# Reordering the Strassen products of a ConvFFN up-projection, and what runs beside them

## The chip, the cores and the metric

The kernel runs on one core of one Trainium2 chip. The metric is the device time of one execution in microseconds (us). The engines are TensorE (PE in the views; PEld is its weight load), VectorE (DVE), ScalarE (ACT), GpSimd (POOL) and SyncE (SP), whose queue issues all the DMA transfers spoken of here. Each engine works through its own instructions in the order in which they stand, and waits at an instruction until what it needs is there.

## The reference, cut to what matters

The whole is one step of a hybrid decoder layer over 1024 prompt tokens and 32 sample tokens (1056 columns). The change touches the last part: the output projection of the cross-attention, the norm before the ConvFFN, its up-projection with a causal depthwise convolution and a SiLU gate, and the down-projection.

```
x = x + cross_attn(rmsnorm(x, norm_xa_w), mem_k, mem_v, xa_w_q, xa_w_o)   # ... @ xa_w_o is "phase e"
def conv_ffn(h, buf, w_up, conv_w, conv_b, w_down):                        # h = rmsnorm(x, norm_ffn_w)
    up = h @ w_up                                                          # 1024 -> 2 * 2816
    up, new_buf = causal_dwconv(up, buf, conv_w, conv_b)                   # width 3
    gate, val = jnp.split(up, 2, axis=-1)
    return (jax.nn.silu(gate) * val) @ w_down, new_buf
x = x + f
y = rmsnorm(x, final_norm_w)
```

## The kernel before, in words

Activations lie with features on the 128 partitions and tokens along the row. Every fp32 product is made of three float32r products: `split` writes a rounded copy (`S.copy`, on ScalarE, L143) and the rest (`V.tensor_tensor`, on VectorE, L144), for weights (`w_raw` into `w_hi` and `w_lo`) and for activations alike.

**Phase e** (`phase_e`, L1394 to L1402) is the output projection, in two halves of the tokens: h = 1 with 544 columns (512 prompt and 32 sample tokens) first, then h = 0 with 512. For each of 8 output tiles m, `gemm` runs 24 matmuls (per piece of at most 512 columns) into a PSUM bank, VectorE adds the bank to the residual `raw` (L1397), ScalarE squares it, VectorE adds the square to `acc` (L268), and the next weight tile is split. Two weight tiles are held at most, so that the third output tile needs the split of its weights.

**Operand sums** (`operands`, L1404 to L1441): the normed half is scaled (L1419) and made into the operands of a Strassen-like product with seven multiplications in place of eight: `B11`, `T1` to `T4`, `B21`, `B22`, each with 4 pieces that are subtracted or added and then split. In the order of the program the calls are `phase_e(1)`, `operands(1)`, `phase_e(0)`, `operands(0)`.

**Up stage**: 22 calls of `up_pair(j)`, each for one tile of the gate and one of the value, 128 features each. A pair has seven steps, one for each product; a step runs 12 matmuls with 272 columns (half 1) and 12 with 256 (half 0). `up_quads` loads the two weight tiles of a pair (`w_raw` with two buffers, and `w_raw2`, named w_raw with a number in the order, with one), builds four weight sums in `ws` (on GpSimd, L1454 to L1459) and splits seven weights. They go by turns to tiles named `w_hi` and `w_lo`, two of each, so that a split waits until the product two back with the same name is done. Products are gathered in PSUM: a pair takes four banks for each half (all eight banks in all); partial results are kept in `c1`, `u2`, `u3`, and `out` writes the four quarters of the pair into `fu` and `fus`. Then the convolution follows (ScalarE L1548 and L1549, VectorE L1551 and L1552), SiLU (L1556), the product of gate and value (L1558), and the write to `h_d` in DRAM.

**Down stage**: `hidden(j)` loads a row tile of `h_d` and splits it; four tiles make a group (groups of 4, 4, 4, 4, 2, 4). `down_all` runs, for each of 8 output tiles m and each of 4 quarters of 264 columns, the matmuls of a group (L1603), and VectorE adds each bank to `x2` (the residual, loaded from DRAM at L1576). The weights come through `weight_tiles` with one tile read ahead.

The order in which instructions of different parts stand in an engine's queue is set by a scheduler from this program; it is shown below where it matters.

## Time and profile before

| what | value |
|---|---|
| median of 3 runs | 2004.17 us (1997.27 to 2010.63) |
| the profiled execution | 2003.78 us, its span 2002.0 us |
| mean granted TensorE clock | 0.97 of full speed |
| instructions | 37716 |

The time of an execution is a little longer than the span of its instructions (here by 1.8 us). Sums below are made against the profiled execution, which lies 0.4 us below the median.

### The profile page before, as it was taken

The numbers are of one execution on the slowest core, as the hardware profiler recorded it, in microseconds if no ns is written. First come the engines' busy times: TensorE is split into PE (matmuls) and PEld (weight loads), VectorE is DVE, ScalarE is ACT, GpSimd is POOL, SyncE is SP. The second block draws the span as 40 slices with busy tenths as digits, with TensorE's granted clock in tenths as the row PEclk, the third lists the DMA queues.
The fourth block names the chain that finished last, engine by engine and source line by source line (L and its number), as shares of the span: only waits on it lengthen the run. The fifth ranks groups of instructions, "written<-read, shape, count | busy, mean of one in ns | idle before, by whom it ended". The sixth has DMA issues, their size and how long they took to land.

```text
span 2002.0 us, 37716 instructions
## 1 busy us (share of the span) xinstructions
PE 1846.5 (92%) x15248; PEld 1632.6 (82%) x15248; DVE 1338.2 (67%) x2711; ACT 790.5 (39%) x1541; POOL 287.9 (14%) x405
## 2 busy tenths in 40 slices
PE   6998999989999999999999787999989999799997
PEld 6887878856777677899768677999889999799997
DVE  5566776777786687556554657777777777655466
ACT  4443334345544445345433324444434344311121
POOL 0021110001110100000000012333333333000001
PEclk9999999979999999999999898999999999899999
DMA  7421113153221223753466231121121122732212
GB/s 255 170 67 41 41 38 107 40 155 128 68 71 51 69 62 110 238 176 127 168 228 213 81 116 50 65 75 65 64 85 66 65 75 71 256 91 87 74 54 88
DMA packets 111599, 207.79 MB, mean 104 GB/s; under 512 B 37760, under 2 KB 51392, under 8 KB 111424
## 3 DMA queue, kind: packets, MB, share of 16 engines
q1 hardware_dynamic: 111424, 205.37, 31.5%
q8 instruction: 120, 1.97, 0.4%
q14 instruction: 55, 0.45, 0.1%
HBM read 166.22 MB, written 39.12 MB: 103 GB/s over the span
## 4 chain that ended last, share of the span: by engine, by line
PE 67%; DVE 13%; issue 7%; ACT 5%; DMA 5%; POOL 2%; SPq 0%; POOLq 0%; ACTq 0%; DVEq 0%
PE ps_g L214 21%; PE ps_m L1527 4%; PE ps_y L214 4%; DVE fo L1551 4%; PE ps_g L1603 3%; PE ps_c L1603 3%; PE ps_g L1527 3%; PE ps_x L1527 2%; PE ps_y L1603 2%; PE ps_c L1527 2%; PE ps_x L1603 2%; ACT fo L1548 1%; POOL ir_r L230 1%; DVE fo L1558 1%; ACT w_hi L143 1%
## 5 line engine op out<-in xcount | busy, mean ns | idle before, releaser
L214 PE MATMUL ps_g<-act,w_hi 128*128 128x272 f32 (+1 forms) x1728 | 428.6, 335 | 3.5 <-DVE raw L1397 3.5
L214 PEld LDWEIGHTS ps_g<-act,w_hi 128*128 128x128 f32 x1728 | 293.6, 192 | 42.2 <-issue 12.2
L143 ACT CAST w_hi<-w_raw 128x1024 fp32r<-128x1024 f32 (+1 forms) x174 | 159.3, 916 | 408.6 <-PE ps_g L214 163.2
L214 PE MATMUL ps_g<-act,w_lo 128*128 128x272 f32 (+1 forms) x864 | 291.2, 337 | 0.3
L144 DVE TENSOR_TENSOR w_lo<-w_raw,w_hi 128x1024 fp32r<-128x1024 f32 (+1 forms) x152 | 168.9, 1111 | 77.9 <-ACT w_hi L143 72.5
L214 PEld LDWEIGHTS ps_g<-act,w_lo 128*128 128x128 f32 x864 | 166.4, 193 | 17.3 <-issue 4.6
L1551 DVE SCALAR_TENSOR_TENSOR fo<-fu,vec,fo 128x1024 f32<-128x1024 f32 x88 | 144.8, 1683 | 10.1 <-ACT fo L1548 10.1
L230 POOL TENSOR_TENSOR ir_r<-ir_v,nhalf 128x8 f32<-128x8 f32 (+3 forms) x20 | 34.0, 1698 | 442.9 <-DVE ir_v L226 399.3
L1527 PE MATMUL ps_m<-act,w_hi 128*128 128x272 f32 x528 | 79.9, 294 | 13.2 <-DVE w_hi L144 12.1
L214 PE MATMUL ps_g<-xq,w_hi 128*128 128x272 f32 (+1 forms) x336 | 88.6, 350 | 0.0
L1527 PEld LDWEIGHTS ps_m<-act,w_hi 128*128 128x128 f32 x528 | 70.3, 190 | 18.1 <-DVE w_hi L144 16.9
L1603 PE MATMUL ps_g<-xq,w_hi 128*128 128x264 f32 x392 | 74.5, 287 | 9.0 <-ACT xq L143 9.0
L1527 PE MATMUL ps_m<-xq,w_hi 128*128 128x256 f32 x528 | 74.2, 283 | 0.0
L1527 PE MATMUL ps_c<-xq,w_lo 128*128 128x272 f32 (+1 forms) x528 | 72.4, 286 | 0.0
L1603 PE MATMUL ps_c<-xq,w_hi 128*128 128x264 f32 x380 | 71.9, 286 | 0.0
L143 ACT CAST w_lo<-ws 128x512 fp32r<-128x512 f32 x22 | 13.7, 621 | 142.5 <-PE ps_c L1527 142.5
L1603 PEld LDWEIGHTS ps_g<-xq,w_hi 128*128 128x128 f32 x392 | 61.9, 191 | 9.2 <-ACT xq L143 9.2
L1527 PE MATMUL ps_x<-xq,w_lo 128*128 128x272 f32 x264 | 40.3, 303 | 30.8 <-DVE u L1534 30.8
L1527 PEld LDWEIGHTS ps_m<-xq,w_hi 128*128 128x128 f32 x528 | 68.3, 191 | 0.0
L1527 PEld LDWEIGHTS ps_c<-xq,w_lo 128*128 128x128 f32 x528 | 68.2, 191 | 0.0
L1454 POOL TENSOR_TENSOR ws<-w_raw 128x512 f32<-128x512 f32 x22 | 45.3, 2061 | 158.0 <-ACT xq L143 156.0
L214 PEld LDWEIGHTS ps_g<-xq,w_hi 128*128 128x128 f32 x336 | 59.2, 194 | 10.1 <-issue 3.3
(634 smaller groups left out, 4450.3 us busy)
## 6 DMA issues: line engine op xcount, KB each, us to landing
w_raw<-i_w_in SPq DMA_DIRECT2D x52, 512.0 KB, 3.3
w_raw<-i_w_up SPq DMA_DIRECT2D x44, 512.0 KB, 3.3
h_d<-fo SPq DMA_DIRECT2D x22, 528.0 KB, 2.6
fo<-h_d SPq DMA_DIRECT2D x22, 528.0 KB, 4.9
w_raw<-i_w_out SPq DMA_DIRECT2D x16, 512.0 KB, 4.4
ck<-i_ck SPq DMA_DIRECT2D x16, 512.0 KB, 4.3
w_raw<-i_xa_w_q SPq DMA_DIRECT2D x16, 512.0 KB, 3.3
ck<-i_cv SPq DMA_DIRECT2D x16, 512.0 KB, 4.3
```

What stands on the lines that cost most here:

```text
L143: S.copy(out=hi, in_=src)
L144: V.tensor_tensor(out=lo, in0=src, in1=hi.bitcast(F32), op=ALU.subtract)
L214: PE.matmul(pt[:, :n], a[:, k], b, start=i == 0, stop=i == 3 * nk - 1)
L230: G.tensor_tensor(out=r[:rows, :n], in0=v[:rows, :n], in1=nhalf[:rows, 0:1].to_broadcast([rows, n]), op=ALU.pow)
L1454: G.tensor_tensor(out=s1, in0=wu[:, 0:4], in1=wu[:, 4:8], op=ALU.add)
L1527: PE.matmul(pt[:, :n], w[:, a], X[name][k][:, b], start=i == 0 and not more, stop=i == 11, skip_group_check=True)
L1548: S.activation(out=o[:, 0:2 * T], in_=ub[i][:, 2:2 + 2 * T], func=AF.Identity, scale=w3[2], bias=vc("fb", mt))
L1551: V.scalar_tensor_tensor(out=o[:, 0:2 * T], in0=ub[i][:, t:t + 2 * T], scalar=w3[t], in1=o[:, 0:2 * T], op0=ALU.mult, op1=ALU.add)
L1558: V.tensor_tensor(out=os_[1], in0=os_[1], in1=os_[0], op=ALU.mult)
L1603: PE.matmul(pt[:, :NW], a[:, k], x[:, b], start=i == 0, stop=i == 3 * n - 1)
```

## The change

Five things are done. (1) The seven products come in another order, B11, B21, T2, T1, T3, T4, B22, and are gathered in three banks for each half: one bank takes B11, T2, T3 and T4 one after the other and ScalarE copies it out after B11, T2 and T3 (`c1`, `u2`, `u3`); B21 and T1 have a bank each, and B22 is added to T1's. (2) The weight sums are made on VectorE, all four `ws` tiles are held. (3) `operands(1)` becomes a generator of which four steps are taken after each output tile of `phase_e(0)`. (4) The sample tokens lie behind the prompt tokens in one `fu` tile, so that the convolution is one instruction of 1072 columns in place of two; the result goes to a tile `fh` of its own. (5) In the last pair `passage` loads and splits the first group of the down stage after steps 0 and 1, and loads `x2` after steps 3 and 4, into the tiles that the products leave. `places` is the list of pools that these tiles are taken from.

```diff
-    NAMES = ("B11", "T2", "T3", "T4", "T1", "B21", "B22")
+    NAMES = ("B11", "B21", "T2", "T3", "T1", "T4", "B22")
...
-        def phase_e(h, oa):
+        def phase_e(h, oa, beside=()):
...
+                for _ in range(4):
+                    next(beside, None)
...
-        def operands(h, raw, root):
+        def operands(h, raw, root, X):
...
-                s1, s2, s3, s4 = (f1.tile([P, 4, P], F32, name="ws", bufs=3) for _ in range(4))
+                s1, s2, s3, s4 = (f1.tile([P, 4, P], F32, name="ws", bufs=4) for _ in range(4))
                 for q in range(7):
-                    if q == 1:
-                        G.tensor_tensor(out=s1, in0=wu[:, 0:4], in1=wu[:, 4:8], op=ALU.add)
-                        G.tensor_tensor(out=s2, in0=s1, in1=wg[:, 0:4], op=ALU.subtract)
...
+                    if q == 2:
+                        V.tensor_tensor(out=s1, in0=wu[:, 0:4], in1=wu[:, 4:8], op=ALU.add)
+                        V.tensor_tensor(out=s2, in0=s1, in1=wg[:, 0:4], op=ALU.subtract)
+                    if q == 3:
+                        V.tensor_tensor(out=s3, in0=wg[:, 0:4], in1=wu[:, 0:4], op=ALU.subtract)
+                        V.tensor_tensor(out=s4, in0=wg[:, 4:8], in1=s2, op=ALU.subtract)
+                    x = (wg[:, 0:4], wg[:, 4:8], s2, s1, s3, wu[:, 4:8], s4)[q]
...
-        X1 = operands(1, raw1, root1)
-        raw0, root0 = phase_e(0, oa0)
-        X0 = operands(0, raw0, root0)
+        raw0, root0 = phase_e(0, oa0, operands(1, raw1, root1, X1))
+        for _ in operands(0, raw0, root0, X0):
+            pass
...
-            pts = [[ps("g") for _ in range(2)] for _ in range(4)]
+            pts = [[ps("g") for _ in range(2)] for _ in range(3)]
...
-(("B11", 0, False), ("T2", 1, False), ("T3", 2, False), ("T4", 2, True), ("T1", 3, False), ("B21", 0, True), ("B22", 3, True))
+(("B11", 1, False), ("B21", 0, False), ("T2", 1, True), ("T1", 2, False), ("T3", 1, True), ("T4", 1, True), ("B22", 2, True))
...
+                    if step_ in (0, 2, 4):
+                        S.copy(out=(c1, u2, u3)[step_ // 2][q], in_=pt[:, :n])
+                    if step_ == 1:
+                        out(0, 0, q, add(c1[q], pt))
                     elif step_ == 4:
-                        out(1, 1, q, add(u3[q], pt))
+                        out(1, 1, q, add(u3[q], pts[2][q]))
                     elif step_ == 5:
-                        out(0, 0, q, copy(pt))
+                        out(1, 0, q, copy(pt))
+                hook(step_)
...
+        def passage(step_):
+
+            if step_ in (0, 1):
+                first.append(hidden(2 * step_))
+                first.append(hidden(2 * step_ + 1))
+            if step_ in (3, 4):
+                for k in range(4 * step_ - 12, 4 * step_ - 8):
+                    t = slot().bitcast(F32).rearrange("p a b -> p (a b)")[:, :NTOK]
+                    nc.sync.dma_start(out=t, in_=x2_d[k])
+                    x2.append(t)
```

**VectorE, at the change from the first half of phase e to the second.** The rows of before, from the norm's root of half 1 on; L1419 scales, L144 splits, L1428 and L1430 are operand sums, and the add of the second half's first output tile (L1397, raw_12155) comes 60 instructions behind the root:

```order
L226 TENSOR_SCALAR ir_v<-ps_c 68x8
L1419 SCALAR_TENSOR_TENSOR raw_11511<-raw_11511,vec,ps_c 128x272
...
L144 TENSOR_TENSOR act<-raw_11834,act 128x272
L144 TENSOR_TENSOR act<-raw_11899,act 128x272
L144 TENSOR_TENSOR act<-raw_11964,act 128x272
L1397 TENSOR_TENSOR raw_12155<-raw_12155,ps_y 128x512
```

The same place now, with L1402 the add of the second half's output tiles and L1427 the scaling:

```order
L226 TENSOR_SCALAR ir_v<-ps_c 68x8
L1402 TENSOR_TENSOR raw_12043<-raw_12043,ps_y 128x512
L1427 SCALAR_TENSOR_TENSOR raw_11511<-raw_11511,vec,ps_c 128x272
...
L144 TENSOR_TENSOR xq<-raw_11704,xq 128x272
L144 TENSOR_TENSOR w_lo<-w_raw,w_hi 128x1024
L1402 TENSOR_TENSOR raw_12119<-raw_12119,ps_g 128x512
L1427 SCALAR_TENSOR_TENSOR raw_11769<-raw_11769,vec,ps_c 128x272
L1427 SCALAR_TENSOR_TENSOR raw_11769<-raw_11769,vec,ps_m 128x272
L268 TENSOR_TENSOR acc<-acc,sq 128x512
```

The first add stands ahead of the operand work, and from then on an add, a weight split and a share of the operand work take turns.

**VectorE, one pair of the up stage, now** (L1567 is the convolution, L1574 and L1575 the product of gate and value, L1533 writes a quarter, L1469 to L1473 are the four weight sums; w_raw_15496 and w_raw_15748 are `w_raw2` of this pair and of the next):

```order
L1567 SCALAR_TENSOR_TENSOR fo<-fu,vec,fo 128x1072 x4
...
L144 TENSOR_TENSOR w_lo<-w_raw_15496,w_lo 128x512
L144 TENSOR_TENSOR w_hi<-ws,w_hi 128x512
L144 TENSOR_TENSOR w_lo<-w_raw,w_lo 128x512
L1469 TENSOR_TENSOR ws<-w_raw_15748 128x512
L1533 TENSOR_TENSOR fu<-u_15628,ps_x 128x272
L1470 TENSOR_TENSOR ws<-ws,w_raw 128x512
L1472 TENSOR_TENSOR ws<-w_raw,w_raw_15748 128x512
L144 TENSOR_TENSOR w_hi<-w_raw,w_hi 128x512
L1533 TENSOR_TENSOR fu<-u_15627,ps_c 128x256
```

The sum L1469 needs the load of `w_raw2` for the next pair, whose buffer is free only after the split of w_raw_15496 three rows ahead of it, and the add of a quarter out of PSUM (L1533) stands behind it. Before, the sums stood on GpSimd, and the adds to c1, u2 and u3 (L1532, L1534) in their place.

**SyncE, from the last pair into the down stage.** Before:

```order
L1584 DMA fo<-h_d 128x1056 x2
L184 DMA w_raw<-i_w_down 128x512 x2
L1559 DMA h_d<-fo 128x1056
L1584 DMA fo<-h_d 128x1056 x8
```

Now (L1585 loads a hidden tile, L1599 x2, L1576 writes h_d):

```order
L184 DMA w_raw<-i_w_down 128x512
L1585 DMA fh<-h_d 128x1056
L1576 DMA h_d<-fh 128x1056
L1585 DMA fh<-h_d 128x1056 x2
...
L1585 DMA fh<-h_d 128x1056
...
L1576 DMA h_d<-fh 128x1056
L1614 DMA o_ffn_p<-fp 128x88
L1615 DMA o_ffn_s<-fs 128x704
L1585 DMA fh<-h_d 128x1056 x2
L184 DMA w_raw<-i_w_down 128x512 x2
```

The four loads of the first group now stand ahead of the last pair's write of h_d; the third and fourth weight tile of the down stage, which stood ahead of that write, stand behind it and behind two more loads.

## Rows read from the trace of the kernel before

**Rows 1.** The page: busy time and share of each engine over the span.

```profile
PE 1846.5 (92%) x15248; PEld 1632.6 (82%) x15248; DVE 1338.2 (67%) x2711; ACT 790.5 (39%) x1541; POOL 287.9 (14%) x405
```

**Rows 2.** Busy time by stretch: start:end, length, busy us (instructions), granted clock, DMA share, GB/s.

```profile
1233.10:1715.25 482.15, 442.87 (x3528) 433.96 (x3527) 364.76 (x566) 196.01 (x357) 176.90 (x248) 1.00 0.21 75
1715.25:1724.00 8.75, 0.00 (x0) 0.00 (x0) 7.57 (x9) 4.78 (x6) 0.00 (x0) 0.77 0.90 319
1724.00:1730.20 6.20, 6.02 (x27) 5.99 (x28) 2.64 (x4) 1.83 (x4) 0.00 (x0) 0.50 0.92 298
1730.20:1745.00 14.80, 14.17 (x116) 13.96 (x116) 12.78 (x25) 7.96 (x14) 0.00 (x0) 1.00 0.85 284
...
1138.20:1153.90 15.70, 0.23 (x1) 0.00 (x1) 14.69 (x41) 9.07 (x25) 0.00 (x0) 0.66 0.00 0
...
1190.20:1233.10 42.90, 31.70 (x183) 27.79 (x182) 32.38 (x75) 16.53 (x43) 8.86 (x14) 0.80 0.13 42
```

**Rows 3.** The chain that ended last: start, length, work; two pairs of the up stage.

```profile
1411.59 2.94 PE ps_g L1527 x24
...
1434.61 2.94 PE ps_g L1527 x24
```

**Rows 4.** Timeline of one pair: start, length, engine, line, operation, [idle before <- releaser].

```profile
1438.52 0.69 DVE L144 TENSOR_TENSOR w_lo<-w_raw,w_lo 128x512 fp32r<-128x512 f32 x1 [1.04 <-ACT w_lo L143]
...
1441.10 2.37 ACT L1548 ACTIVATE fo<-fu,vec 128x1024 f32<-128x1024 f32 x2
...
1442.38 5.43 DVE L1551 SCALAR_TENSOR_TENSOR fo<-fu,vec,fo 128x1024 f32<-128x1024 f32 x3 [0.46 <-ACT fo L1548]
...
1443.37 2.16 POOL L1454 TENSOR_TENSOR ws<-w_raw 128x512 f32<-128x512 f32 x1
...
1443.68 0.63 ACT L1530 COPY c<-ps_g 128x272 f32<-128x272 f32 x2
...
1449.98 1.52 PE L1527 MATMUL ps_m<-act,w_hi 128*128 128x272 f32 x10 [0.43 <-DVE w_hi L144]
...
1453.34 1.77 PE L1527 MATMUL ps_x<-xq,w_lo 128*128 128x272 f32 x12 [1.49 <-DVE u L1534]
```

**Rows 5.** DMA issues of the up stage (1300 to 1690): size, median us to landing.

```profile
w_raw<-i_w_up SPq DMA_DIRECT2D x33, 512.0 KB, 3.3
h_d<-fo SPq DMA_DIRECT2D x17, 528.0 KB, 2.6
```

**Rows 6.** Timeline and, for the last row, chain: second half of phase e, operands, first pair.

```profile
1128.48 0.50 DVE L1419 SCALAR_TENSOR_TENSOR raw<-raw,vec,ps_c 128x272 f32<-128x272 f32 x1 [2.62 <-PE ps_c L252]
...
1153.11 0.67 DVE L1397 TENSOR_TENSOR raw<-raw,ps_y 128x512 f32<-128x512 f32 x1
...
1153.71 1.21 DVE L144 TENSOR_TENSOR w_lo<-w_raw,w_hi 128x1024 fp32r<-128x1024 f32 x1
...
1153.93 1.19 PE L214 MATMUL ps_y<-xq,w_hi 128*128 128x512 f32 x2 [15.50 <-DVE raw L1397]
...
1190.31 0.69 DVE L1397 TENSOR_TENSOR raw<-raw,ps_g 128x512 f32<-128x512 f32 x1 [3.11 <-PE ps_g L214]
...
1197.04 1.41 DVE L1419 SCALAR_TENSOR_TENSOR raw<-raw,vec,ps_c 128x512 f32<-128x512 f32 x2 [1.84 <-PE ps_c L252]
...
1218.17 0.68 DVE L144 TENSOR_TENSOR w_hi<-ws,w_hi 128x512 fp32r<-128x512 f32 x1
...
1184.67 5.61 PE ps_g L214 x24
```

**Rows 7.** Timeline: from the last pair into the down stage.

```profile
1716.87 2.45 SPq L184 DMA_DIRECT2D w_raw<-i_w_down  x2
1717.11 3.68 DVE L1551 SCALAR_TENSOR_TENSOR fo<-fu,vec,fo 128x1024 f32<-128x1024 f32 x3 [0.52 <-ACT fo L1548]
...
1723.70 0.33 SPq L1559 DMA_DIRECT2D h_d<-fo  x1
...
1724.18 0.81 PE L1603 MATMUL ps_g<-xq,w_hi 128*128 128x264 f32 x2 [8.97 <-ACT xq L143]
```

More of the change, by code (lines that the diff above doesn't have):

```diff
@@ L1425, in operands @@
                 put("B11", k, lo[k])
+                yield
             for k in range(4):
                 scale(4 + k)
+                put("B21", k, lo[4 + k])
+                yield
+            for k in range(4):
                 V.tensor_tensor(out=hi[k], in0=hi[4 + k], in1=hi[k], op=ALU.subtract)
-                put("T3", k, hi[k])
                 V.tensor_tensor(out=lo[k], in0=lo[k], in1=hi[k], op=ALU.add)
                 put("T2", k, lo[k])
+                yield
+                put("T3", k, hi[k])
+                yield
             for k in range(4):
@@ L1434, in operands @@
                 put("T1", k, hi[k])
+                yield
+            for k in range(4):
                 V.tensor_tensor(out=lo[k], in0=lo[4 + k], in1=lo[k], op=ALU.subtract)
                 put("T4", k, lo[k])
-            for k in range(4):
-                put("B21", k, lo[4 + k])
+                yield
             for k in range(4):
                 put("B22", k, hi[4 + k])
-            return X
+                yield
         def up_quads():
@@ L1477, in pf_ @@
         def pf_():
[L1478 removed]
+            return ff.tile([P, NU], F32, name="fu", bufs=2)[:, :400]
         fp = ff.tile([P, 44, 2], F32, name="fp")
@@ L1518, in copy @@
                 return op
-            for step_, (name, bank, more) in enumerate((("B11", 0, False), ("T2", 1, False), ("T3", 2, False), ("T4", 2, True), ("T1", 3, False), ("B21", 0, True), ("B22", 3, True))):
+            for step_, (name, bank, more) in enumerate((("B11", 1, False), ("B21", 0, False), ("T2", 1, True), ("T1", 2, False), ("T3", 1, True), ("T4", 1, True), ("B22", 2, True))):
                 w = next(quads)
@@ L1557, in up_pair, with hidden, slot @@
                 os_.append(o)
-            V.tensor_tensor(out=os_[1], in0=os_[1], in1=os_[0], op=ALU.mult)
-            nc.sync.dma_start(out=h_d[j], in_=os_[1])
+            hj = ff.tile([P, NTOK], F32, name="fh", bufs=2)
+            V.tensor_tensor(out=hj[:, 0:2 * T], in0=os_[1][:, 0:2 * T], in1=os_[0][:, 0:2 * T], op=ALU.mult)
+            V.tensor_tensor(out=hj[:, 2 * T:].rearrange("p (b t) -> p b t", t=4), in0=samples_of(os_[1]), in1=samples_of(os_[0]), op=ALU.mult)
+            nc.sync.dma_start(out=h_d[j], in_=hj)
+        NW = NTOK // 4
+        LAST = tuple((i * NW, NW) for i in range(4))
+        x2, first = [], []
+        def hidden(j):
+            o = ff.tile([P, NTOK], F32, name="fh", bufs=2)
+            nc.sync.dma_start(out=o, in_=h_d[j])
+            hh = [slot()[:, :, :2 * NW] for _ in range(2)]
+            for i in range(2):
+                split(hh[i][:, 0], hh[i][:, 1], o[:, 2 * NW * i:2 * NW * i + 2 * NW])
+            return hh
+        def passage(step_):
[7 more added lines that the diff above has]
+                    x2.append(t)
+            if step_ == 6:
+                weights[0] = weight_tiles(down_sources())
+        ga = [xp_tile] * 2 + [act_tile] * 2 + [xp_tile] * 2 + [xe_tile] * 2
+        gb = [xp_tile] * 4 + [act_tile] * 4
+        places = ga + [xp_tile] * 2 + [xe_tile] * 2 + [act_tile] * 2 + [xp_tile] * 2 + gb + ga + gb + ga[:4] + gb
+        def slot():
+            return places.pop(0)()
         for j in range(FT):
-            up_pair(j)
+            up_pair(j, passage if j == FT - 1 else lambda i: None)
         nc.sync.dma_start(out=O["ffn_p"], in_=fp)
@@ L1566, in hybrid_step @@
         rings.update(g="ggyccx", m="mm")
-        weights[0] = weight_tiles(down_sources())
-        slots = [xp_tile, act_tile]
-        def slot():
-            slots.append(slots.pop(0))
-            return slots[-1]()
-        x2 = []
-        for k in range(KT):
-            t = act_tile().bitcast(F32).rearrange("p a b -> p (a b)")[:, :NTOK]
-            nc.sync.dma_start(out=t, in_=x2_d[k])
-            x2.append(t)
-        NW = NTOK // 4
-        LAST = tuple((i * NW, NW) for i in range(4))
-        def hidden(j):
-            o = ff.tile([P, NTOK], F32, name="fo", bufs=4)
-            nc.sync.dma_start(out=o, in_=h_d[j])
-            hh = [xp_tile()[:, :, :2 * NW] for _ in range(2)]
-            for i in range(2):
-                split(hh[i][:, 0], hh[i][:, 1], o[:, 2 * NW * i:2 * NW * i + 2 * NW])
-            return hh
         def hcols(hh, q):
@@ L1618, in hybrid_step @@
             j0 = sum(GR[:g])
-            hs_ = [hidden(j) for j in range(j0, j0 + gn)]
+            hs_ = [hidden(j) for j in range(j0, j0 + gn)] if g else first
             if prev:
```

42 lines of the change are left out of this document (17 added, 25 removed).

## The prediction

> **What bounds the kernel now.** I read the page first: TensorE is busy for 92% of the span, VectorE for 67%, GpSimd for 14% [rows 1]. So a gain can only come out of the 8% in which TensorE stands still, or runs at less than its full clock; I looked for these in the table by stretch [rows 2], and then in the timeline of the places that stand out.
>
> Three places stand out. From the 60% mark on, one pair of the up stage follows another at a steady 482.15 / 21 = 22.96 us with the clock granted in full [rows 2]. The chain shows a step's 24 matmuls in 2.94 us [rows 3], so seven steps need 20.58 us, and 2.38 us of each pair are waits: 0.43 us for a weight split on VectorE and 1.49 us for the add into u3 on VectorE (T4 may not be gathered into the bank before T3 is read out of it), the rest being slow restarts [rows 4]. Both waits end on VectorE, which at that time is in its convolution. Ahead of that, in the second half of phase e, TensorE stands still for 15.50 us at the third output tile: the adds and weight splits that it needs stand behind all of the first half's operand work in VectorE's queue, which runs from 1128.48 to 1153.11 [rows 6], and nothing of TensorE's runs beside it (0.23 us of 15.70) [rows 2]. Last, the way into the down stage: 8.75 us without a matmul, then 6.20 us at a granted 0.50, the 1.2 GHz level [rows 2].
>
> **The change, part by part.**
>
> *Operand sums beside phase e.* VectorE's work does not get less, its order changes. The split of the third weight tile (1153.71 now [rows 6]) moves behind one add, eight scalings and four splits; at 0.35 to 0.5 us each that is 6 us behind 1128.5, so 1134.7, and TensorE's third tile starts 19 us earlier. From there on either engine can be the limit. TensorE's limit: six tiles at 5.61 [rows 6] are 33.7 us, so that the last add would start at about 1169.5 in place of 1190.31: a gain of 20.8. VectorE's limit: the operand work with its waits, 24.6 us, eight adds and eight square sums at 0.67, six splits at 1.21, and the first five of the up stage's sums and splits, at 0.69 [rows 4, 6], are 46.1 us from 1127.8 on, so 1173 for the last add: a gain of 17. The two are so near that they will wait for each other now and then; I take 18.5, and 14 to 21 for the range. The wait added to VectorE's queue, of the very first sum for the load of `w_raw2` in front of phase e, costs nothing: behind it stand the last splits of the attention, and phase e's first adds have their own loads to wait for.
>
> *The first pair.* From the scaling of half 0 (1197.04) to the end of the operand work it is 21.1 us [rows 6], and the same afterwards. From then on the first pair now takes until 1233.1, 14.9 us, in a stretch granted 0.80 [rows 2]. In the new order T1 and T3 can run while T4's and B22's operands are still made, so that two products are left, 5.9 us at full clock; I expect the 1.2 GHz level for a part of it, as now, and 10 us. Gain 5; 0 and 9 are the bounds.
>
> *Up stage, TensorE.* Let t count from a pair's first matmul. T2 (t = 5.9) may be gathered into its bank once ScalarE has copied B11's sum out: ScalarE has two convolution instructions of 1.2 us first, and is through with both copies by t = 4.1. T3 comes 2.9 us after T2, with T1 between. T4 follows T3 directly: its half 1 needs the copy of half 1, made beside T3's half 0 by t = 13.9 (needed at 14.7), its half 0 the copy that stands behind one weight cast, at t = 15.7 (needed at 16.2). So the 1.49 goes, and what is late next has 0.5 us to spare. The copies are 0.3 us each [rows 4], and ScalarE has the room: 196.01 of 482.15 us busy [rows 2].
>
> The Trainium skill, "PSUM — Partial Sum Buffer", section "PSUM bank collisions raise a hardware error", asks that an engine's access to a bank be kept apart from TensorE's by semaphores, bank by bank: with T2, T3 and T4 in one bank each must wait for ScalarE's copy. The wait of 1.49 before T4 is such a one in this trace. By that rule alone the wait stays, only for another engine, and what it would give is the first rival.
>
> *Up stage, VectorE.* It loses two adds for each half (1.6 us), the four short convolution instructions (1.0), and the hindrance by GpSimd: three convolution instructions take 5.43 us while GpSimd makes its sums, and 3.68 in the last pair where it makes none [rows 4, 7], so 1.75. It gains four sums of 128x512, as long as a split of that size, 0.69 [rows 4], 2.8 us at most, and 0.5 us for the wider instructions. From 364.76 / 21 = 17.4 busy [rows 2] it comes to 16.3 of 20.6. It would fit; what matters is its order. The split of the last weight out of `w_raw2` is reached at t = 10.8 (convolution from 2.3 to 7.4, a split, the product, three adds). Only then can the next `w_raw2` be loaded, and 3.3 us after its issue [rows 5], at t = 14.6, the first sum can start. VectorE stands there for 1.4 us with the two adds behind it that B22 waits for. By t = 15.8 and 18.2 both are done; B22's halves need them at 17.6 and 19.1. So a second margin of 0.9 us. TensorE is then not held up anywhere: 20.58 us, 20.65 with a little loss, and 21 pairs give 21 x 2.31 = 48.5. The bounds are 50 (no loss at all) and 25 (half the present wait comes back, 1.1 us, as the rows of the waits show it for one of the two).
>
> *Into the down stage.* Here now 8.75 us without work, 2.9 us by the half clock (27 matmuls in 6.20, where the next row has 116 in 14.17, 0.122 each, so 3.3) and 0.7 us later are lost, 12.35 in all [rows 2]. The change loads the first group early, but a tile `fh` has two buffers, which the h_d writes use too. The second tile's load waits for the write of the pair before (t = 9.7 and 2.6 for the landing [rows 5]), the fourth for the split of the second, at t = 19, and lands 2.5 us after the pair's end. TensorE starts at once, stops some 2 us for the fourth tile, and runs on for the first two output tiles, until 13 us after the pair's end. The third needs weights whose load now stands behind the write of h_d (after the convolution, which the fourth tile's splits hold up: 11 us after the pair's end) and behind a load into the buffer of that write (14.4), where it stood ahead of it (at 1716.87 against 1723.70 [rows 7]). With the landing, the two hidden tiles ahead of it on ScalarE, and its own split, it is ready some 20.5 us after the pair's end. So TensorE stands for 2 and 8 us, and runs slow for a while behind the long stop as it does now, 3 us: 13, against 12.35 lost now. I take a loss of 1 us; the bounds are a gain of 9.4 (all hidden but 3 us) and a loss of 5.
>
> The Trainium skill, "SBUF — State Buffer", section "Summary: rules for kernel authors", puts a transfer out of DRAM at about 358 GB/s. This trace has 284 to 319 GB/s here, at 0.85 to 0.92 of the queues' time [rows 2]; by the page's figure the loads would land about a sixth sooner and the sum would be, as an estimate, 2 us lower. I go by the trace.
>
> The sample columns laid behind the prompt's and the tile `fh` are in the sums of VectorE above; the end of the kernel is not touched.
>
> **The sum.** 18.5 + 5 + 48.5 - 1 = 71, off 2003.8: 1933 us. Against the median of the runs it is the same within 0.4 us.
>
> **The rivals.**
>
> *The wait for a bank or for `w_raw2` stays.* For it speaks that both margins are under 1 us, and that a wait on a load which comes 1 us late is paid in full in every pair. Against it, that every pair begins anew at TensorE's end, so that no lateness adds up. With 1.0 to 1.5 us a pair it is 21 to 31 us less gain: 1954 to 1964. Chance 0.17.
>
> *The way into the down stage is hidden after all*, because the loads land sooner or weights come in time: 9.4 us gained in place of 1 lost, 1922. For it: first group, x2 and two weight tiles are in hand when the pair ends. Against: the place of the third weight's load. Chance 0.13.
>
> *VectorE cannot keep up in phase e.* It has 46 us of work for some 45 us of matmuls there; if each step waits for ScalarE as in the rows of before, or TensorE's clock falls again, half of the gain is left: 1943. Chance 0.09.
>
> *Slower than before.* One mechanism: the next `w_raw2` has only one buffer and is loaded only after t = 10.8; if in the up stage it lands late, VectorE stands with B22's adds behind it and TensorE stops in every pair. The point from which it decides: the rest of the change gains 22.5, so a pair would have to take 24.0, 3.4 us over TensorE's 20.6; with the margin of 0.9 and the 3.3 of now, the load would need 7.6 us. At 9 us it would be 2003.8 - 22.5 + 21 x 2.4 = 2032. Nothing in the up stage is so slow (3.3, with a DMA share of 0.21 [rows 2, 5]). Chance 0.03.
>
> **How the numbers follow.** The forecast, 1924 to 1943, has 0.58; the rivals 0.17, 0.13, 0.09 and 0.03. A range of 1920 to 1957 holds the forecast's case, the case of the hidden way in, that of phase e, and a third of the first rival's, some 8 in 10. A measurement of this kernel tells a difference of about 1%, 20 us. Faster by more than that are all the cases but the last, and the worst of the first: 0.95; within 1%: 0.02; slower: 0.03.
>
> **What would show it.** In the changed kernel a pair should take 20.6 to 20.7 us, with PE busy throughout and no wait on a bank; VectorE should show one idle time of 1 to 2 us in a pair that ends with the load of w_raw2, and GpSimd nearly nothing. Phase e's second half should run without a stop of more than 2 us and its last add fall near 1172. Behind the last pair there should be a stop at the third output tile of the down stage that ends with a weight cast on ScalarE, 20 us after the pair's end. Wrong would make it a pair of 21.5 us or more, a stop in phase e, or a way into the down stage without a stop.

## The result, and the profile after

The changed kernel took 1946.81 us (median of 4 runs, 1922.29 to 1949.68), the kernel before 2001.37 beside it: a ratio of 0.969, 95% interval 0.961 to 0.978. The profiled execution is the one of 1922.29 us, granted 0.975 on the mean; the other three lay at 1945 to 1950 with a granted 0.961 to 0.964, and none of them left a trace. Repeated twice, on two chips, the same kernel took 1920.20 (1917.62 to 1923.61, 6 runs; ratio 0.959, 0.956 to 0.962) and 1921.32 us (1917.13 to 1924.80, 6 runs; 0.957, 0.954 to 0.961). So the steps below are read from executions of 1920 to 1923 us, and the 25 us of those three runs are a question of their own.

The page, busy time by engine, to be held against [rows 1]:

```profile
PE 1829.3 (95%) x15248; PEld 1623.6 (85%) x15248; DVE 1293.5 (67%) x2645; ACT 810.2 (42%) x1585; POOL 191.6 (10%) x317
```

The table by stretch, to be held against [rows 2]: the second half of phase e, the first pair's slow part, the 21 further pairs, and three stretches behind the last pair.

```profile
1127.40:1168.80 41.40, 39.97 (x178) 31.82 (x176) 39.99 (x84) 21.45 (x44) 0.00 (x0) 1.00 0.37 121
...
1184.00:1192.60 8.60, 8.55 (x26) 6.24 (x26) 8.50 (x26) 5.45 (x14) 0.00 (x0) 0.50 0.00 1
...
1203.40:1635.10 431.70, 431.70 (x3531) 431.70 (x3529) 328.06 (x508) 216.76 (x404) 90.66 (x169) 1.00 0.24 82
1635.10:1647.20 12.10, 12.10 (x98) 11.68 (x96) 11.04 (x17) 5.15 (x6) 0.00 (x0) 1.00 0.88 349
1647.20:1655.40 8.20, 0.01 (x2) 0.01 (x1) 2.84 (x5) 2.91 (x6) 0.00 (x0) 0.73 0.87 288
1655.40:1664.00 8.60, 8.60 (x48) 8.41 (x49) 5.40 (x10) 3.43 (x6) 0.00 (x0) 0.66 0.86 280
```

A pair takes 431.70 / 21 = 20.56 us with TensorE busy throughout. In the second half of phase e TensorE and VectorE are both busy for 97% of the time. Behind the last pair TensorE runs on for 12 us, then stands for 8.2. The chain of waits, here at the end of phase e and at two steps of a pair, holds hardly anything but matmuls in both places:

```profile
1147.00 10.68 PE ps_g L214 x46
1157.68 5.55 PE ps_y L214 x24
1163.23 5.56 PE ps_g L214 x24
1168.81 0.69 DVE raw L1402
...
1230.00 2.93 PE ps_m L1548 x24
1232.93 2.94 PE ps_g L1548 x24
```

The timeline of one pair (a pair begins at 1388.42; the first four rows belong to the end of the one ahead of it):

```profile
1381.69 0.69 DVE L1469 TENSOR_TENSOR ws<-w_raw 128x512 f32<-128x512 f32 x1 [0.54 <-DMA w_raw<-i_w_up]
1382.30 0.43 DVE L1533 TENSOR_TENSOR fu<-u,ps_c 128x272 f32<-128x272 f32 x1
...
1383.27 0.37 ACT L1551 COPY u<-ps_g 128x256 f32<-128x256 f32 x1
...
1384.45 0.41 DVE L1533 TENSOR_TENSOR fu<-u,ps_y 128x256 f32<-128x256 f32 x1
...
1390.50 5.07 DVE L1567 SCALAR_TENSOR_TENSOR fo<-fu,vec,fo 128x1072 f32<-128x1072 f32 x4 [0.50 <-ACT fo L1565]
...
1398.82 0.33 SPq L1465 DMA_DIRECT2D w_raw<-i_w_up  x1
```

Counted from a pair's start, `w_raw2` is issued at t = 10.4, VectorE's first sum begins at 13.8 behind a wait of 0.54 (0.88 on the mean of 19 waits, 16.8 us in all), and the two adds that B22 waits for end at 14.9 and 17.0. ScalarE's last copy, for T4, ends at 15.8. Four convolution instructions take 5.07 us where three took 5.43 [rows 4]. The timeline of the way into the down stage, against [rows 7]:

```profile
1645.39 0.32 SPq L1576 DMA_DIRECT2D h_d<-fh  x1
...
1647.11 1.33 SPq L1585 DMA_DIRECT2D fh<-h_d  x2
...
1648.49 0.98 SPq L184 DMA_DIRECT2D w_raw<-i_w_down  x2
1651.47 1.16 ACT L143 CAST xq<-fh 128x528 fp32r<-128x528 f32 x2 [9.38 <-DMA fh<-h_d]
...
1654.73 1.13 ACT L143 CAST w_hi<-w_raw 128x512 fp32r<-128x512 f32 x2
...
1655.39 0.81 PE L1631 MATMUL ps_y<-xq,w_hi 128*128 128x264 f32 x2 [8.19 <-ACT w_hi L143]
```

It is the forecast's picture: SyncE issues the write of h_d, two hidden tiles, then the weights, ScalarE casts the hidden tiles ahead of the weights, and TensorE waits for that last cast.

### The profile page after: what moved, and what is told of

Read it like the earlier page. It is cut to its first block, busy times and chain, and to the rows that moved or that the text cites. A ratio compares the mean times of both kernels' runs of the same rounds, so it can differ in the third digit from the quotient of the medians.

```text
span 1920.3 us, 37453 instructions
## 1 busy us (share of the span) xinstructions
PE 1829.3 (95%) x15248; PEld 1623.6 (85%) x15248; DVE 1293.5 (67%) x2645; ACT 810.2 (42%) x1585; POOL 191.6 (10%) x317
## 4 chain that ended last, share of the span: by engine, by line
PE 80%; DVE 6%; DMA 5%; ACT 4%; POOL 2%; issue 2%; SPq 0%; POOLq 0%; DVEq 0%; ACTq 0%
PE ps_g L214 22%; PE ps_g L1548 6%; PE ps_c L1548 6%; PE ps_m L1548 6%; PE ps_y L214 4%; PE ps_c L1631 4%; PE ps_g L1631 3%; PE ps_y L1548 3%; PE ps_x L1548 3%; PE ps_y L1631 2%; PE ps_x L1631 2%; POOL ir_r L230 1%; PE ps_m L532 1%; PE ps_x L605 1%; ACT w_hi L143 1%
## 5 line engine op out<-in xcount | busy, mean ns | idle before, releaser
L214 PEld LDWEIGHTS ps_g<-act,w_hi 128*128 128x128 f32 x1728 | 291.3, 191 | 42.1 <-issue 11.9
L144 DVE TENSOR_TENSOR w_lo<-w_raw,w_hi 128x1024 fp32r<-128x1024 f32 (+1 forms) x152 | 168.5, 1109 | 75.2 <-ACT w_hi L143 69.8
L1567 DVE SCALAR_TENSOR_TENSOR fo<-fu,vec,fo 128x1072 f32<-128x1072 f32 x88 | 111.7, 1329 | 10.4 <-ACT fo L1565 10.4
L214 PE MATMUL ps_g<-xq,w_hi 128*128 128x272 f32 (+1 forms) x336 | 86.2, 342 | 0.9 <-ACT w_hi L143 0.9
L214 PEld LDWEIGHTS ps_g<-xq,w_hi 128*128 128x128 f32 x336 | 57.1, 188 | 10.6 <-issue 3.3
L1513 POOL COPY fu<-sst 128x16 f32<-128x16 f32 x44 | 64.0, 1469 | 0.0
L214 PE MATMUL ps_g<-xq,w_lo 128*128 128x272 f32 (+1 forms) x168 | 57.4, 342 | 0.0
L1565 ACT ACTIVATE fo<-fu,vec 128x1072 f32<-128x1072 f32 x44 | 54.2, 1276 | 0.0
L144 DVE TENSOR_TENSOR w_lo<-w_raw,w_lo 128x512 fp32r<-128x512 f32 x44 | 30.1, 685 | 31.4 <-ACT w_lo L143 31.4
L1548 PE MATMUL ps_c<-xq,w_hi 128*128 128x272 f32 (+1 forms) x348 | 49.2, 290 | 0.0
L144 DVE TENSOR_TENSOR w_hi<-ws,w_hi 128x512 fp32r<-128x512 f32 x66 | 45.2, 684 | 5.6 <-ACT w_hi L143 5.5
L214 PE MATMUL ps_y<-xq,w_hi 128*128 128x512 f32 (+1 forms) x176 | 47.9, 353 | 0.5 <-ACT w_hi L143 0.5
L1548 PE MATMUL ps_g<-xq,w_hi 128*128 128x272 f32 (+1 forms) x348 | 46.6, 286 | 0.0
L1548 PEld LDWEIGHTS ps_c<-xq,w_hi 128*128 128x128 f32 x348 | 45.9, 193 | 0.2 <-ACT w_hi L143 0.2
```

What stands on the lines that cost most here:

```text
L144: V.tensor_tensor(out=lo, in0=src, in1=hi.bitcast(F32), op=ALU.subtract)
L214: PE.matmul(pt[:, :n], a[:, k], b, start=i == 0, stop=i == 3 * nk - 1)
L1513: G.tensor_copy(out=us_[i][:, :, 0:2], in_=sst[:, mt])
L1548: PE.matmul(pt[:, :n], w[:, a], X[name][k][:, b], start=i == 0 and not more, stop=i == 11, skip_group_check=True)
L1565: S.activation(out=o, in_=ub[i][:, 2:NU], func=AF.Identity, scale=w3[2], bias=vc("fb", mt))
L1567: V.scalar_tensor_tensor(out=o, in0=ub[i][:, t:t + NU - 2], scalar=w3[t], in1=o, op0=ALU.mult, op1=ALU.add)
```

## The experiments

| run | median, us | a pair, us | first up matmul at | last pair to end |
|---|---|---|---|---|
| before (first trace) | 2001.37 | 22.96 | 1190.1 | 286.8 |
| after (the changed kernel) | 1946.81 | 20.56 | 1168.6 | 285.2 |
| again | 1920.20 | 20.56 | 1172.0 | 283.3 |
| again_2 | 1921.32 | 20.56 | 1169.5 | 285.0 |
| sums_gpsimd | 1925.92 | 20.59 | 1172.3 | 284.5 |
| old_order | 1931.66 | 20.71 | 1180.5 | 289.5 |
| old_both | 2007.40 | 23.75 | 1181.5 | 291.3 |
| before_sums | 1949.28 | 20.72 | 1186.8 | 285.5 |
| not_beside | 1943.33 | 20.56 | 1189.8 | 284.9 |
| passage_behind | 1926.84 | 20.56 | 1177.7 | 288.2 |
| weights_first | 1918.66 | 20.56 | 1169.6 | 281.4 |
| weights_ahead | 1918.61 | 20.56 | 1189.0 | 274.8 |
| weights_ahead_2 | 1913.89 | 20.57 | 1169.7 | 274.9 |
| copy_thrice | 1928.46 | 20.98 | 1172.8 | 279.4 |

A pair is the time of the last 21 pairs divided by 21; the last three columns are of the one profiled execution, and the last column runs from the end of the last pair to the end of the kernel.

**The same kernel again.** No edit.

> The changed kernel once more, unchanged, to see where its runs of 1945 to 1950 us lose what the profiled one of 1922 us does not. The granted clock of those runs is 0.961 to 0.964 against 0.975. Theory 1 (the clock in the stage that now has no stop): part of the up stage is granted half the clock in such a run, some 50 us of it, and a profile of one shows pairs of up to 41 us between pairs of 20.6. Theory 2 (the old places): the up stage stays at 20.56 us a pair and 1.00, and the loss lies in stretches that stop and go, ahead of phase e and behind the last pair. Either way the median should be 1922 to 1950 us.

> The changed kernel once more, as the measure for the three runs beside it: 1917 to 1924 us as in its first repetition, or up to 1950 us where an execution loses time ahead of phase e. One profiled execution of another kernel lost 17 us there, in a stretch of 44.4 us at half clock some 460 us from the start, where its code is that of the changed kernel.

Twelve runs of 1917 to 1925 us, none at 1945, so neither theory met the executions it was made for. A trace with such a loss came from another kernel, weights_ahead, whose profiled execution took 1930.44 us; its first up matmul lies 19 us later than in the second run of the same code (weights_ahead_2), and its pairs take 20.56 us at a clock granted in full. So the loss lies ahead of the up stage. The table by stretch of that execution, and then of the profiled one of weights_ahead_2:

```profile
440.00:450.00 10.00, 10.00 (x32) 4.43 (x32) 8.38 (x16) 4.73 (x8) 0.00 (x0) 0.88 0.26 74
450.00:460.00 10.00, 10.00 (x20) 3.46 (x18) 4.24 (x7) 1.95 (x3) 0.00 (x0) 0.50 0.61 179
460.00:480.00 20.00, 20.00 (x39) 7.54 (x39) 7.34 (x13) 4.25 (x9) 0.00 (x0) 0.50 0.31 85
```

```profile
440.00:450.00 10.00, 10.00 (x36) 4.26 (x36) 8.39 (x16) 4.73 (x8) 0.00 (x0) 1.00 0.23 65
450.00:460.00 10.00, 10.00 (x35) 4.11 (x33) 7.07 (x12) 4.62 (x7) 0.00 (x0) 1.00 0.76 246
460.00:480.00 20.00, 18.73 (x97) 11.88 (x97) 13.83 (x35) 13.21 (x36) 0.61 (x4) 0.91 0.28 95
```

From the same matmul (L1117) to the same later one (L1156) the first takes 57.4 us and the second 38.7, which is nearly the whole difference. That is Theory 2's kind of place, in a part that the change does not touch. The profiled executions of old_order (1946.56 us) and passage_behind (1934.08 us) lie above their medians too, and their first up matmul comes 6 to 12 us later than in the three traces of the changed kernel. That the runs of 1945 to 1950 us lost their time ahead of the up stage is likely, not shown.

**The weight sums on GpSimd again** (sums_gpsimd), **the old order of the products** (old_order), **both** (old_both).

```diff
-                        V.tensor_tensor(out=s1, in0=wu[:, 0:4], in1=wu[:, 4:8], op=ALU.add)
+                        G.tensor_tensor(out=s1, in0=wu[:, 0:4], in1=wu[:, 4:8], op=ALU.add)
...
-(("B11", 1, False), ("B21", 0, False), ("T2", 1, True), ("T1", 2, False), ("T3", 1, True), ("T4", 1, True), ("B22", 2, True))
+(("B11", 0, False), ("T2", 1, False), ("T3", 2, False), ("T4", 2, True), ("T1", 3, False), ("B21", 0, True), ("B22", 3, True))
...
+                    elif step_ == 2:
+                        V.tensor_tensor(out=u3[q], in0=u2[q], in1=pt[:, :n], op=ALU.add)
```

> The changed kernel with its four weight sums back on GpSimd, all else as it is. Theory A (the order of the products on three banks carries the gain of a pair): GpSimd takes 4 x 2.16 us from the landing of w_raw2 at t = 14 on, so the last sum is ready at t = 22.6 and the first that a product needs 12 us ahead of it; a pair stays at 20.6 to 20.8 us and the time within 5 us of the changed kernel. Theory B (VectorE freed of GpSimd carries it): the convolution takes 1.81 us an instruction again in place of 1.33, a wait on VectorE comes back, a pair takes 21.5 us or more, 20 us or more in all.

> The changed kernel with the old order of the products on four banks for each half, with the two adds into u2 and u3 on VectorE, but with the weight sums on VectorE and the wide convolution; the first group of the down stage is loaded behind the last pair, as before. Theory A (the order carries the gain): T4 waits again for VectorE's add into u3, 1 to 1.5 us, and the pair takes 21.5 to 22.9 us, 20 to 49 us more in all. Theory B (VectorE freed of GpSimd carries it): the add is in time, a pair takes 20.6 to 20.9 us, and the time is within 10 us of the changed kernel. If both parts are needed, this one and the one with the sums on GpSimd are both slower by 20 us or more.

> The old order of the products on four banks and the weight sums on GpSimd, all else as in the run with the old order alone (wide convolution, operand sums beside phase e, first group of the down stage loaded behind the last pair). Either of the two undone alone left the pair at 20.56 and some 20.7 us. If each is enough by itself (the wait on VectorE is shorter than what either takes away), with both undone the pair goes back to 22 to 23 us, 27 to 47 us more than the run with the old order alone. If neither carries the gain, but the wide convolution or another part does, the pair stays at 20.6 to 21.2 us, within 10 us of that run.

In old_order and old_both the first group of the down stage is also loaded behind the last pair, not in it; that touches what follows the pairs, not the pairs. Each part undone alone leaves the pair nearly as it was, 20.59 and 20.71 us. In time, sums_gpsimd and old_order are 6 and 11 us above the changed kernel on the same chip, each about 1 us more than the 5 and 10 us that their theories allowed; in old_order's trace the stretch behind the last pair is 6 us longer (289.5 against 283.3). Both undone bring a pair of 23.75 us, more than the 22.96 of before; why more is open. Theory A failed on the old order, Theory B on the sums; the third expectation's first case holds, by more than it said (76 us): either is enough, and what one of them could gain was already gained with the other. The table by stretch over the 21 pairs, and TensorE's longest wait (us in all, times, longest), of the kernel with both undone:

```profile
1223.77:1722.44 498.67, 444.24 (x3530) 435.57 (x3528) 368.77 (x502) 184.05 (x314) 208.52 (x248) 1.00 0.19 67
```

```profile
PE ps_x L1549 <- DVE u L1556: 39.5, 19, 2.1
```

The wait for the add into u3 (L1556) is back, 2.1 us a pair, and the timeline of one pair shows why:

```profile
1463.92 7.15 DVE L1572 SCALAR_TENSOR_TENSOR fo<-fu,vec,fo 128x1072 f32<-128x1072 f32 x4 [0.49 <-ACT fo L1570]
1464.11 2.30 POOL L1469 TENSOR_TENSOR ws<-w_raw 128x512 f32<-128x512 f32 x1 [2.79 <-DMA w_raw<-i_w_up]
...
1466.48 2.21 POOL L1470 TENSOR_TENSOR ws<-ws,w_raw 128x512 f32<-128x512 f32 x1
...
1471.75 2.20 POOL L1472 TENSOR_TENSOR ws<-w_raw,w_raw 128x512 f32<-128x512 f32 x1
...
1472.73 1.27 DVE L1580 TENSOR_TENSOR fh<-fo 128x32 f32<-128x32 f32 x1
```

Two sums of GpSimd lie beside the convolution, which takes 7.15 us in place of 5.07, and a third beside the product of gate and value, whose last 32 columns take 1.27 us in place of 0.22. The add into u3 stands behind both on VectorE, so it comes some 3 us late, and TensorE waits 2.1 of them. With the new order the same sums stand elsewhere (timeline of sums_gpsimd):

```profile
1384.65 0.44 DVE L1533 TENSOR_TENSOR fu<-u,ps_c 128x272 f32<-128x272 f32 x1 [0.57 <-ACT u L1551]
1384.72 1.30 POOL L1469 TENSOR_TENSOR ws<-w_raw 128x512 f32<-128x512 f32 x1 [4.54 <-DMA w_raw<-i_w_up]
...
1386.11 1.29 POOL L1470 TENSOR_TENSOR ws<-ws,w_raw 128x512 f32<-128x512 f32 x1
...
1386.32 1.62 DVE L144 TENSOR_TENSOR w_hi<-w_raw,w_hi 128x512 fp32r<-128x512 f32 x1 [1.23 <-ACT w_hi L143]
...
1389.06 1.29 POOL L1473 TENSOR_TENSOR ws<-w_raw,ws 128x512 f32<-128x512 f32 x1
...
1393.43 5.07 DVE L1567 SCALAR_TENSOR_TENSOR fo<-fu,vec,fo 128x1072 f32<-128x1072 f32 x4 [0.49 <-ACT fo L1565]
```

All four are over before the convolution begins, since the new order lets `w_raw2` go, and so be loaded, earlier in its pair (at t = 10.4, with both undone at 22.7). Three of the sums take 1.29 or 1.30 us there, the third 1.75, and the convolution its 5.07. What they meet there instead is two weight splits, of 1.62 and 1.37 us in place of 0.68; TensorE does not come to wait for these.

**One part alone, on the kernel before** (before_sums).

```diff
-                        G.tensor_tensor(out=s1, in0=wu[:, 0:4], in1=wu[:, 4:8], op=ALU.add)
-                        G.tensor_tensor(out=s2, in0=s1, in1=wg[:, 0:4], op=ALU.subtract)
+                        V.tensor_tensor(out=s1, in0=wu[:, 0:4], in1=wu[:, 4:8], op=ALU.add)
+                        V.tensor_tensor(out=s2, in0=s1, in1=wg[:, 0:4], op=ALU.subtract)
...
-                        G.tensor_tensor(out=s3, in0=wg[:, 0:4], in1=wu[:, 0:4], op=ALU.subtract)
+                        V.tensor_tensor(out=s3, in0=wg[:, 0:4], in1=wu[:, 0:4], op=ALU.subtract)
...
-                        G.tensor_tensor(out=s4, in0=wg[:, 4:8], in1=s2, op=ALU.subtract)
+                        V.tensor_tensor(out=s4, in0=wg[:, 4:8], in1=s2, op=ALU.subtract)
```

> The kernel before with one change alone: its four weight sums on VectorE in place of GpSimd. The runs with one part undone say that in the up stage either part is enough. Then this one alone takes the pair from 22.96 to 20.6 to 21.2 us, with convolution instructions of about 1.27 us in place of 1.70 and no wait for the add into u3, 37 to 50 us less than the kernel before: 1952 to 1966 us. If it is enough only together with the wide convolution (the four short instructions are still there) or with VectorE's other relief, the pair stays above 21.8 us and less than 25 us are gained.

1949.28 us (1945.29 to 1957.84), a ratio of 0.972 (0.968 to 0.976): four engine names bring 53 of the 81 us, and the time lies 3 us below the range expected. By the traces 47 us of the gain lie in the 21 pairs. The table by stretch over 21 pairs, and the convolution's group, of the kernel before and then of this one:

```profile
1226.90:1661.94 435.04, 435.04 (x3530) 433.05 (x3528) 364.51 (x646) 197.05 (x356) 66.38 (x167) 1.00 0.24 83
```

```profile
L1551 DVE SCALAR_TENSOR_TENSOR fo<-fu,vec,fo 128x1024 f32<-128x1024 f32 x81 | 134.4, 1697 | 9.1 <-ACT fo L1548 9.1
```

```profile
L1551 DVE SCALAR_TENSOR_TENSOR fo<-fu,vec,fo 128x1024 f32<-128x1024 f32 x80 | 98.9, 1277 | 0.0
```

An instruction takes 1277 ns against 1697, and TensorE waits for nothing in a pair of 20.72 us. No run undid the wide convolution by itself; this kernel has the narrow one and the old order, so against the 20.56 of the changed kernel the two together are worth at most 0.16 us a pair once the sums are moved.

**The operand sums ahead of phase e's second half again** (not_beside).

```diff
-        raw0, root0 = phase_e(0, oa0, operands(1, raw1, root1, X1))
+        for _ in operands(1, raw1, root1, X1):
+            pass
+        raw0, root0 = phase_e(0, oa0)
```

> The changed kernel with the operand sums of half 1 made ahead of the second half of phase e again, not beside it. By the step of the forecast, as the trace of the changed kernel has it, the last add of phase e comes 20 us later (1190 against 1169) with a stop of about 15 us at the third output tile, and nothing else changes: 18 to 23 us slower. The rival: what the interleaving gives at phase e, it takes from the first pair, whose operands for half 0 would then be the only ones left to make in either case, and the first pair in a slower clock takes a part back: 8 to 14 us slower.

23 us slower (1943.33 against 1920.20, on the same chip), the upper end of the first theory. The stop is back (timeline), the first up matmul comes 18 us later than in again and 21 later than in the first trace, and the first pair takes nothing back (34.3 us in this run, 34.4 in again):

```profile
1154.63 1.19 PE L214 MATMUL ps_y<-xq,w_hi 128*128 128x512 f32 x2 [15.40 <-DVE raw L1402]
```

**The margin of ScalarE's copy** (copy_thrice). The kernel makes the copy into u3 three times; no value changes.

```diff
-                        S.copy(out=(c1, u2, u3)[step_ // 2][q], in_=pt[:, :n])
+                        for _ in range(3 if step_ == 4 else 1):
+                            S.copy(out=(c1, u2, u3)[step_ // 2][q], in_=pt[:, :n])
```

> The changed kernel in which ScalarE copies T3's bank out three times (the same copy into u3 again), so that the bank comes free for T4 some 0.75 us later; the copies repeat and alter no value. By the forecast's margin (the copy of half 0 ends at t = 16.0, T4 needs the bank at 16.2) TensorE then waits 0.5 to 0.9 us for ScalarE in each pair: a pair of 21.1 to 21.5 us and 11 to 19 us more in all, with the wait at T4's first matmul. If the margin was wider than the steps said, the pair stays at 20.6 us and the time within 4 us.

The pair takes 20.98 us, 0.42 more, and the time is 7 to 8 us more: too much was expected, with a copy done at t = 16.0 where the forecast has 15.7. The copy of half 0 takes 1.18 us in place of 0.37, so 0.39 of the 0.81 more were margin, as the trace after has it (copy done at t = 15.8, bank needed at 16.2). T4's halves start 0.06 and 0.05 us behind the ends of the copies (timeline):

```profile
1408.44 1.22 ACT L1552 COPY u<-ps_m 128x272 f32<-128x272 f32 x3 [0.89 <-PE ps_m L1548]
...
1409.72 1.75 PE L1548 MATMUL ps_m<-act,w_lo 128*128 128x272 f32 x12
...
1410.40 1.18 ACT L1552 COPY u<-ps_m 128x256 f32<-128x256 f32 x3
...
1411.63 1.70 PE L1548 MATMUL ps_m<-xq,w_lo 128*128 128x256 f32 x12
```

So the wait for the bank is there, as the Trainium skill, "PSUM — Partial Sum Buffer", section "PSUM bank collisions raise a hardware error", asks for it; in the changed kernel it ends 0.4 us before TensorE needs the bank. In this run the way into the down stage is 4 to 6 us shorter (last column), which hides half of the loss in the time. SyncE's queue shows what shortened it (timeline):

```profile
1642.54 0.33 SPq L184 DMA_DIRECT2D w_raw<-i_w_down  x1
...
1657.16 0.32 SPq L1577 DMA_DIRECT2D h_d<-fh  x1
```

The scheduler has set the third weight tile's load ahead of the last write of h_d, where the changed kernel issues it behind that write (1648.49 and 1645.39). TensorE's stops behind the last pair add up to 3.8 us in place of 8.2, with no edit made there.

**The way into the down stage**: the early loads taken back (passage_behind), the third weight tile ahead of the second group's hidden tiles (weights_first), and its load also ahead of the last write of h_d (weights_ahead, twice).

```diff
-            up_pair(j, passage if j == FT - 1 else lambda i: None)
+            up_pair(j)
+        for i in range(7):
+            passage(i)
```

```diff
...
                     w = wnext()
+                if m == 1:
+                    got = [hidden(j) for j in more]
...
```

```diff
...
-                weights[0] = weight_tiles(down_sources())
+                weights[0] = weight_tiles(down_sources(), 1)
+                first_w.append(wnext())
...
```

The second diff is cut from the loop over the output tiles: the next group's hidden tiles (`more`) are called behind the second tile's weights. The last is of `passage`, step 6: one weight tile is taken there, with one raw tile read further ahead; weights_ahead has both.

> The changed kernel with the first group of the down stage and x2 loaded and split behind the last pair, not beside it. By the forecast's step (the early loads move the stop, they do not take it away) the stops behind the last pair add up to about the same, some 8 us ahead of the first matmul and 3 to 4 us at the next hidden tiles or weights against the 8.2 of the changed kernel: 1 to 6 us more in all. The rival (the early loads hide the way in): 9 us or more.

> The changed kernel with one shift on the way into the down stage: the loads and splits of the second group's hidden tiles are called behind the second output tile's weights, not ahead of the whole group, so that the load and the cast of the third weight tile stand ahead of them on SyncE and ScalarE, but still behind the last write of h_d. If the stop of 8.19 us at the third output tile is the place of that load in the queue, as the forecast says: the load goes out at about 1646.6 in place of 1648.5 and its cast needs to wait for no hidden tile, so the tile is ready at about 1651 in place of 1655.4 and the stop is 3 to 4.5 us, 4 to 7 us less in all with the shorter slow stretch behind it. If the loads themselves are too slow (the queues are busy for 0.82 to 0.87 of the time there), the stop stays at 7 to 9 us, only with another load at its end.

> The same shift, and the third weight tile's load one tile further ahead and ahead of the last write of h_d. If the stop at the third output tile is a matter of place alone: the raw weights lie there before the second output tile ends, the split waits only for the weight buffers of the first, the stop is 0 to 1.5 us, and the stretch at half clock behind it (10.2 us of the profiled run) goes with it: 8 to 14 us less than the changed kernel, 1906 to 1914 us. If something else holds the stage up there (the transfers themselves, VectorE behind the last convolution), the stop moves to the fourth output tile or the second group and 5 us or less are gained.

> The kernel with the third weight tile's load ahead of the last write of h_d, once more. Its profile had one stop of 0.96 us behind the last pair in place of 8.19, no slow stretch there, and 274.9 us from the last pair to the end in place of 283.4 to 285.4; but its executions were spread from 1910 to 1938 us by what happens ahead of phase e. If the 9 to 10 us of that stage are real, the median is 8 to 11 us below the changed kernel beside it; if the stage gives them back elsewhere, within 4 us of it.

TensorE's stops behind the last pair in the timelines, of passage_behind, weights_first and weights_ahead_2:

```profile
1651.65 0.81 PE L1633 MATMUL ps_g<-xq,w_hi 128*128 128x264 f32 x2 [7.40 <-ACT xq L143]
...
1653.28 0.59 PE L1633 MATMUL ps_g<-xq,w_hi 128*128 128x264 f32 x1 [0.51 <-DVE xq L144]
...
1659.39 0.52 PE L1633 MATMUL ps_g<-act,w_hi 128*128 128x264 f32 x2 [2.62 <-ACT act L143]
```

```profile
1652.43 0.81 PE L1631 MATMUL ps_y<-xq,w_hi 128*128 128x264 f32 x2 [4.38 <-ACT w_hi L143]
```

```profile
1648.97 0.51 PE L1639 MATMUL ps_y<-xq,w_hi 128*128 128x264 f32 x2 [0.52 <-ACT w_hi L143]
```

Without the early loads the stops add up to 10.5 us, where the three traces of the changed kernel have one stop of 8.2, 7.3 and 8.5; the stage is 3 to 5 us longer, and the median lies 5.5 us above the changed kernel beside it, within the 1 to 6 expected. The change moved the stop, it did not remove it. The place of one weight load is worth the rest: a stop of 4.4 us in weights_first, 1.0 and 0.5 in the two runs of weights_ahead, and a stage of 281.4 and 274.8 to 274.9 us where the changed kernel has 283.3 to 285.2. The stop of weights_first came as expected (3 to 4.5), the time did not: 1918.66 us is 1.5 to 2.7 below the changed kernel's two repetitions, where 4 to 7 were expected, and that is not clear of their spread. The first run of weights_ahead missed too (1918.61 us, with 1906 to 1914 expected); its 1910.11 to 1938.19 hold the execution described above. The median of the second is 1913.89 us (1911.01 to 1921.51), 7.4 below the changed kernel beside it, where 8 to 11 were expected and the stage gives 10.2; five of its six runs lie below all six of that kernel. It is the fastest version here, 0.954 of the kernel before (0.950 to 0.958).

## Why the prediction was right

The time measured first (1946.81) and the repeated ones (1920.20, 1921.32) lie 14 us above and 12 to 13 below the 1933 forecast. That the first lies no further off is partly luck: three of its four executions hold a loss of some 25 us that the sum does not know, and the sum itself is 11 us short of the gain. By the trace the difference of the two spans, 81.7 us, falls into these pieces:

| piece | forecast | trace |
|---|---|---|
| phase e, second half, to its last add | 18.5 | 20.6, and 0.9 ahead of it |
| from there to the end of the first pair | 5 | 1.0 + 7.2 |
| 21 pairs | 48.5 | 50.5 |
| into the down stage and on to the end | -1 | 1.5 |

The two parts of the second row are from the last add to the scaling of half 0, which the forecast left out, and from there to the end of the first pair.

*Phase e.* TensorE's third tile started at 1134.42 (1134.7 was said). The step that was off is VectorE's limit: it counted 46.1 us of work from the first add to the last, and the trace has 41.4 (1127.38 to 1168.81), 1.4 of them idle. The five sums and splits of the up stage do stand ahead of the last add, as it said, the last of them here (timeline):

```profile
1167.93 0.68 DVE L1473 TENSOR_TENSOR ws<-w_raw,ws 128x512 f32<-128x512 f32 x1
```

Counted too high were the operand work, taken with the 2.4 us of waits that it has in the kernel before (22.2 us without them, before and after), and the adds and squares: thirteen, not sixteen, stand ahead, and each holds up the next instruction for 0.60 us, not 0.67. So TensorE's limit held, 20.8, and 18.5 was taken too low. The rival that VectorE cannot keep up was near: both engines were 97% busy, and TensorE waited twice, 0.48 and 0.94 us, for a cast.

*First pair.* The slow stretch came (0.50 from 1184.00 to 1192.60); the 7.2 us are 2 us above the forecast's 5 and inside its bounds.

*Up stage.* The pair and the copy's margin came as worked out; the wait for `w_raw2` was shorter (0.88 us on the mean, 1.4 said), and the adds for B22 ended about 1 us earlier than said. GpSimd, of which nearly nothing was expected, is busy for 4.3 us of a pair. What the step got wrong is its reason: it let the 1.49 us go by the new order alone, and put the 1.75 us of hindrance by GpSimd only into VectorE's busy time, where they decide nothing. They are two ways out of one wait: the add into u3 is late because the convolution ahead of it is late, and the convolution is late because GpSimd's sums run beside it. Moving the sums takes away the cause, the new order takes away the add; the runs show each alone within 0.2 us a pair of both together. The first rival's waits of 1.0 to 1.5 us did not come.

*Into the down stage.* Instead of a loss of 1 us there was a gain of 1.5, mainly because the fourth hidden tile held up the weight loads by 0.21 us only (2 said). The rest came as said: a stop of 8.19 for the third weight tile (8 said), with the cast done 20.3 us behind the pair's end (20.5 said), then 48 matmuls in 8.60 us where 98 had taken 12.10: 2.7 lost (3 said). The order of the queues was enough to place this stop, and weights_ahead to remove it. The transfers moved 349 GB/s there (1635.10 to 1647.20), near the 358 that the Trainium skill, "SBUF — State Buffer", section "Summary: rules for kernel authors", gives and above the 284 to 319 that the sum went by; as the stop was a matter of place, that was worth little.

## What to carry to other kernels

Before a wait is given a remedy, follow it one step further back: behind "TensorE waits for VectorE" stood GpSimd, and four engine names alone gave two thirds of what the whole change gave. When a change has several parts, undo each alone and then together; here the new order and the moved sums each look nearly worthless when undone alone, and undone together they cost 76 to 81 us more than either. A transfer that is brought forward helps only if what is needed after it is brought forward too: the twelve tiles loaded early won 3 to 5 us of the stage, the next weight tile's load in its right place some 10 more.

## What the runs showed of the hardware

A sum of GpSimd and an instruction of VectorE that takes two tiles out of SBUF cost each other time where they meet: the convolution took 1.79 us against 1.27 to 1.33, the sum 2.2 to 2.3 against 1.29. They go nearly one after the other: beside two sums the four convolutions took 7.15 us, and one after the other the six would take 5.07 + 2 x 1.29 = 7.65. The one that begins second waits for the other to end: the 32-column product took 1.27 us in place of 0.22 and ended 0.05 us behind the sum that had begun 1 us ahead of it, and the split shown in sums_gpsimd took 1.62 us in place of 0.68 behind a sum that began 0.21 us ahead and kept its 1.29. An add that takes one of its inputs out of PSUM (L1533 there) took its usual 0.44 us beside a sum of 1.30. The Trainium skill, "SBUF — State Buffer", section "SBUF: two separate sides", says that an instruction of VectorE with two SBUF inputs and one of GpSimd that reads SBUF share a pair of ports, which the first to start holds to its end while the other stands still; these rows agree.

The granted clock can stay at its lower level (0.50, 1.2 GHz) though TensorE is busy: in the execution of weights_ahead shown above it was 0.88 on the mean from 440 to 450 and then 0.50 from 450 to 480, with 30.00 of 30 us busy, where the other execution was granted 1.00 and then 0.91. Both had come out of the same stop shortly before (5.16 us up to 427.88, and 5.17 up to 430.55). What makes the one differ from the other is open.
